# Heavy experts on quarters of TensorE's columns, in unsplit float32

## The chip, the cores and the metric

The kernel runs on one core of one Trainium2 chip. The metric is the device time of one execution in microseconds (us); lower is better. The core has TensorE (PE, matrix products), VectorE (DVE), ScalarE (ACT), GpSimd (POOL) and SyncE (SP, which here issues every DMA). TensorE writes to PSUM, which has eight banks of 128 rows by 512 float32.

## What is computed

Two layers of a transformer trunk over 256 latent and 256 context tokens of width 1024. The second layer ends in a mixture of eight experts, and the change lies there alone. In short:

```
logits = h @ router                       # h: 256 x 1024, eight logits a token
top_v, top_i = top_k(logits, 2)           # two experts a token
gates = softmax(top_v), put at top_i
for e in range(8):                        # w_gate, w_up: 1024 x 3584, w_down: 3584 x 1024
    out += gates[:, e:e+1] * ((silu(h @ w_gate[e]) * (h @ w_up[e])) @ w_down[e])
x = x + g2 * out;   return rms_norm(x, final_norm_g)
```

All arrays are float32. One expert's weights are 44 MB, all eight 352 MB; each is read once from HBM. With the inputs of `setup_inputs()` the reference routes 49, 84, 60, 51, 58, 61, 72 and 77 tokens to experts 0 to 7.

## The kernel before

The kernel first runs the mixer and the dense feed-forward part of layer 0, then the mixer of layer 1, then the expert stage (`moe`). The expert stage is the second half of the span.

**Places.** The eight experts are taken in eight places, `KIND = "LHLHHLHL"`. Place 0 is expert 0; the other experts are ranked by their number of tokens when the router's result is known, and ranks 1 to 4 go to the heavy places (H), the others to the light ones (L). A light place has 64 slots for tokens, a heavy one 128 (`CAP`). If an expert has more tokens than slots, `overflow` runs all experts a second time for the rest, in a branch at the end (`tc.If(n > 0)`, line 2390) that is otherwise jumped over by every engine. `slots` makes one-hot matrices of tokens against slots, and `gather` multiplies the tokens with them.

**Weights.** Loads are units of 1 MB, 42 for an expert, issued in order by SP, each into four slots of an arena of 104 slots (`SLOT`, `SLOTS`). The inner width of 3584 is cut into blocks of 1024, 1024, 1024 and 512 columns (`WIDE = (2, 2, 2, 1)`). For each block the gate and up products run over eight steps k of the contraction, the products are combined, transposed by TensorE (`flip`), and `down` multiplies them with rows of w_down into the banks `y`.

**Light places** multiply the float32 weights as they lie in the arena (`native`, `pairs`): the 64 slots are the stationary operand, the gate product goes to rows 0 to 63 of a bank, that is to the left half of the array's columns, and the up product to rows 64 to 127, the right half:

```
self.mm(p[0:64], xs[k], wg(kk, q), k == 0, k == KT - 1)
self.mm(p[64:128], xs[k], wu(kk, q), k == 0, k == KT - 1)
```

A float32 product shows in the trace as two MATMUL records.

**Heavy places** split every weight into a high and a low part in the short type float32r (`wunit`, `cut_next` on ScalarE, `cut_rest` on VectorE), likewise the tokens and the hidden block, and make three products of 128 columns each for one float32 product (`lin`: high by high, high by low, low by high). A split piece takes four more slots of the arena (up to `PIECES = 4` pieces at a time), and a load's slots come free when its split is done.

**Order.** The order on each engine is written by a planner (`drive`) that steps generators by prices of instructions (`mm`) and by the arena's free slots: `place_raw` admits a load while `held_raws * 4 + cut * 4 + live + 4 <= SLOTS - SPARE[self.ap]`, with `SPARE = (16, 26, 26)`. At run time the engines keep this order and wait for each other by semaphores; a load waits until the last reader of its slots is done.

**After an expert**, `slot_gates` puts the gates on the slots, `scaled` multiplies them onto `y` and splits the result, and `combine` spreads it back to the tokens with two products for each of four tiles.

Of the kernel before, what the change touches and what calls it, by code (L numbers as in the profile page):

```python
# [41 lines left out]
SLOT, SLOTS, FOURS, SPARE, ROOM = 512, 104, (5, 3), (16, 26, 26), 62  # L42
# [8 lines left out]
KIND, CAP = "LHLHHLHL", dict(H=128, L=64)  # L51
RANK = (0, 1, 5, 2, 3, 6, 4, 7)
WIDE = (2, 2, 2, 1)
# [81 lines left out]
class Arena:  # L135
# [18 lines left out]
    def take(self, n, dt=F32):  # L154
        i = len(self.uses)
        self.uses.append([n, self.count, self.count, dt == F32R])
        if self.rehearsal:
            s, self.top = self.top, self.top + n
            t = self.all[:, s * SLOT:(s + n) * SLOT].bitcast(dt)
        else:  # L160
            s, new = self.layout[i]
            four = s // 4
            if new:
                t = self.tiles[four] = self.pool.tile([128, 4 * SLOT], dt, name=f"four{four}", tag=f"four{four}")
                self.base[t.tensor.name] = four * 4, 4 * SLOT
            t = self.tiles[four][:, s % 4 * SLOT:(s % 4 + n) * SLOT]
        for k in range(n):
            self.at[s + k] = i
        return t


def lay_out(uses):
# [4 lines left out]
    for n, a, b, r in uses:  # L177
# [5 lines left out]
    for i in sorted(range(len(uses)), key=lambda i: (uses[i][1], -uses[i][0])):  # L183
        n, a, b, r = uses[i]
# [27 lines left out]
class Trunk:  # L212
# [37 lines left out]
    def act(self, dt=F32, name="a", n=1):  # L250
        self.live += n
        self.peak = max(self.peak, self.live)
        return self.arena.take(n, dt)
# [81 lines left out]
    def mm(self, out, lhsT, rhs, start=True, stop=True):  # L335
# [127 lines left out]
    def native(self, src, kts, cols):  # L463
# [3 lines left out]
        def w(k, q=0):  # L467
            c = k * cols + q * 512
            return u["raw"][:, c:c + 512]
# [56 lines left out]
    def load(self, u):  # L526
        u["raw"] = self.arena.take(4)
# [44 lines left out]
    def cut_next(self):  # L572
# [3 lines left out]
        p["h"], p["l"] = self.arena.take(2, F32R), self.arena.take(2, F32R)  # L576
# [238 lines left out]
    def mloads(self):  # L815
        while self.mfree and self.mnext < len(self.mseq):
            l, part, hf, k = self.mseq[self.mnext]
            t = self.arena.take(1)
# [996 lines left out]
    def moe_units(self):  # L1815
# [4 lines left out]
        def make(W, e, r, c, lie, ks):  # L1820
# [3 lines left out]
            w = self.native(src, kts, cols) if KIND[e] == "L" else self.wunit([src], kts, cols)  # L1824
# [3 lines left out]
        def gu(e, i):  # L1828
# [3 lines left out]
            two = [(w, g) for w in range(2) for g in range(0, KT, kts)]  # L1832
            if KIND[e] == "L":
                two.sort(key=lambda x: x[1])
            for w, g in two:
# [4 lines left out]
        def dn(e, i):  # L1840
            f0, n = sum(WIDE[:i]) * 512, WIDE[i] * 512
            us = [make(Dn, e, s(f0, f0 + n), s(0, D), "(p k) c -> p k c", s(g, g + 2)) for g in range(0, n // 128, 2)]
            return [(u, k) for u in us for k in range(2)]
# [141 lines left out]
    def slots(self, e, r=None, pe=None):  # L1985

        t = (self.OH if r is None else self.OHR)[e] = self.act(name="OH")
        io = self.io128
        if KIND[e] == "L":
            io = io[:, 0:64].unsqueeze(1).to_broadcast([128, 2, 64])  # L1990
        for tb in range(2):
            o = t[:, tb * 128:(tb + 1) * 128]
            if KIND[e] == "L":
                o = o.rearrange("p (a s) -> p a s", a=2)
            at = self.pe[:, tb, e:e + 1] if pe is None else pe[:, tb]
            if r is None:
                self.V.tensor_scalar(o, io, at, None, op0=OP.is_equal)
            else:
                self.V.tensor_scalar(o, io, at, r[:, tb:tb + 1], op0=OP.is_equal, op1=OP.mult)
# [8 lines left out]
    def gather(self, e, g, xe):  # L2008

        heavy = KIND[e] == "H"  # L2010
        n, ks = (128, range(g * 4, g * 4 + 4)) if heavy else (64, range(KT))
        p = self.ps("pxe")
        for i, k in enumerate(ks):
            for tb in range(2):
                self.mm(p[:, i * n:(i + 1) * n], self.xtok[tb][k // 4][:, (k % 4) * 128:(k % 4 + 1) * 128],
                        self.OHR[e][:, tb * 128:tb * 128 + n], tb == 0, tb == 1)
        last = not heavy or g == 1
        u = self.act(name="u")
        sl = [slice(i * n, (i + 1) * n) for i in range(len(ks))]
        col = [(self.modc[:, 1, 0, 3, k:k + 1], self.nA[:, 1, 1, 0, k:k + 1]) for k in ks]  # L2020
        v3 = lambda t: t.rearrange("p (k n) -> p k n", n=n)
        wide = lambda t: t.unsqueeze(2).to_broadcast([128, len(ks), n])
        hl = (self.act(F32R, "xeh"), self.act(F32R, "xel")) if heavy else None

        def scale():
            self.V.tensor_mul(v3(u), v3(p), wide(self.nA[:, 1, 1, 0, ks[0]:ks[0] + len(ks)]))
            self.V.tensor_add(v3(u), v3(u), wide(self.modc[:, 1, 0, 3, ks[0]:ks[0] + len(ks)]))
            if last:
                self.drop(1)

        def high():
            if e:
                self.S.copy(hl[0], u)
            else:
                for c, (sh, sc) in zip(sl, col):
                    self.S.activation(hl[0][:, c], p[:, c], AF.Identity, bias=sh, scale=sc)

        def low():
            self.V.tensor_sub(hl[1], u, hl[0].bitcast(F32))
            self.drop(1)  # L2040

        st = [(self.V, scale)]
        if heavy:
            st = (st + [(self.S, high)] if e else [(self.S, high)] + st) + [(self.V, low)]
        self.after(self.t + 196.0, *st, key=("xe", e, g), banks=1)
        xe += [(hl[0][:, c], hl[1][:, c]) if heavy else u[:, c] for c in sl]

    def slot_gates(self, e):

        p = self.ps("pgs")  # L2050
        for tb in range(2):
            self.mm(p[:, e:e + 1], self.OH[e][:, tb * 128:(tb + 1) * 128], self.gate[:, tb, e:e + 1], tb == 0, tb == 1)
        self.after(self.t + 196.0, (self.V, lambda: self.V.tensor_copy(self.gs[:, e:e + 1], p[:, e:e + 1])),
                   key=("gs", e), banks=1)

    def scaled(self, e, Y):

        g, ys = self.gs[:, e:e + 1], []
        if e == NE - 1:
            t = self.act(name="yg")  # L2060
            self.V.scalar_tensor_tensor(t, Y[0], g, self.g2l, op0=OP.mult, op1=OP.mult)
            return [(t,)] * 2

        def split(y, hh, hl):
            def free():
                self.V.scalar_tensor_tensor(hl, y, g, hh.bitcast(F32), op0=OP.mult, op1=OP.subtract)
                self.held -= 1
            return [(self.S, lambda: self.S.activation(hh, y, AF.Copy, scale=g)), (self.V, free)]

        for i, y in enumerate(Y):  # L2070
            hh, hl = self.act(F32R, "yh"), self.act(F32R, "yl")
            ys.append((hh, hl))
            self.after(self.t + 196.0, *split(y, hh, hl), key=("ys", e, i))
        return ys if len(ys) == 2 else ys * 2

    def combine(self, e, ys, hf, tb):

        p = self.ps("pcb")
        rows = slice(0, 128) if KIND[e] == "H" else slice(hf * 64, hf * 64 + 64)
        o = self.OHT[e][rows, tb * 128:(tb + 1) * 128]  # L2080
        if len(ys[hf]) == 1:
            self.mm(p, o.bitcast(F32), ys[hf][0][rows], True, True)
        else:
            self.mm(p, o, ys[hf][0][rows], True, False)
            self.mm(p, o, ys[hf][1][rows], False, True)
        if not e:
            self.tok[tb][hf] = self.act(name="tok")
        t = self.tok[tb][hf]
        if e == NE - 1:
            self.V.tensor_add(t, p, t)  # L2090
            return
        self.after(self.t + 196.0, (self.V, lambda: self.V.tensor_add(t, p, t)) if e else (self.S, lambda: self.S.copy(t, p)),
# [8 lines left out]
    def moe(self, J, R):  # L2101
# [14 lines left out]
        def to_oht(e):  # L2116
            p = self.ps("pot")
            for tb in range(2):
                c = slice(tb * 128, (tb + 1) * 128)
                self.tr(p[:, c], self.OH[e][:, c])  # L2120
            self.OHT[e] = self.act(F32R, "OHT")
            self.after(self.t + 196.0, (S, lambda: S.copy(self.OHT[e][:, 0:256], p[:, 0:256])), key=("oht", e), banks=1)
# [13 lines left out]
        wide = lambda name, j: [(name, j, q) for q in range(WIDE[J[j][1]])]  # L2136
        side = []
        self.gs = C.tile([128, 8], F32, name="gslot")
# [406 lines left out]
```

## Time and profile before

| | us |
|---|---|
| median of 3 runs | 1745.29 (1745.13 to 1747.17) |
| the profiled execution | 1749.87 |
| its span, first to last instruction | 1748.1 |
| TensorE busy | 1707.2 (98%) |
| VectorE busy | 1153.9 (66%) |
| ScalarE busy | 811.9 (46%) |

The profile's pages cut the span into 40 slices, so a slice is 43.7 us, and name a tile by the pool that it comes from: `four` is any piece of the arena, and `g`, `u`, `y`, `pht`, `pcb` are PSUM banks. Nearly every instruction has line 121, that of the recording helper, so groups are told apart by tile and shape. A shape 128*64 on TensorE is 128 rows by 64 columns of stationary operand. The expert stage's products run from 878 to 1734 us.

### The profile page before, as it was taken

To read this page: it belongs to the slowest core of one execution; us is meant where nothing else is said; L and a number is where in the kernel's file an instruction comes from. 1 tells how busy PE (TensorE), PEld (TensorE's weight loads), DVE (VectorE), ACT (ScalarE), POOL (GpSimd) and SP (SyncE) were. 2 spreads that over 40 slices of the span, in tenths; PEclk is the share of its full clock that TensorE was granted. 3 is DMA by queue.
4 is the path that set the end of the run, shared out by engine and by line. 5 is a ranking of instruction groups with operands and counts; after the bars stand their busy time and mean duration, and the time that the engine had idled before them with its cause. 6 is when DMAs were issued, how large, how long until landed. Compare 5 with 4: busy or idle time off the path is not lost. (4 is left out here: it accounts for less than half of the span.)

```text
span 1748.1 us, 22827 instructions
## 1 busy us (share of the span) xinstructions
PE 1707.2 (98%) x8291; PEld 1224.1 (70%) x8291; DVE 1153.9 (66%) x1928; ACT 811.9 (46%) x1388; POOL 1.1 (0%) x7
## 2 busy tenths in 40 slices
PE   8999998999999999999999999999999999999997
PEld 4876777788888888977834787446887864568632
DVE  6898988888874335588512796227999952489523
ACT  3467754433222223466402675126777741367412
POOL 0000000000000000000000000000000000000000
PEclk9899999999999998999989999999999999999999
DMA  9631244455883225116779999999999999999995
GB/s 306 209 120 53 79 139 139 146 172 179 290 289 97 83 76 173 63 59 217 265 291 410 375 374 369 414 407 413 409 366 349 390 356 413 409 411 409 392 411 232
DMA packets 191573, 469.97 MB, mean 269 GB/s; under 512 B 13632, under 2 KB 81756, under 8 KB 177116
## 3 DMA queue, kind: packets, MB, share of 16 engines
q1 hardware_dynamic: 191452, 468.42, 71.9%
q8 instruction: 67, 1.10, 0.3%
q14 instruction: 54, 0.44, 0.1%
HBM read 467.34 MB, written 1.05 MB: 268 GB/s over the span
## 5 line engine op out<-in xcount | busy, mean ns | idle before, releaser
L121 DVE TENSOR_TENSOR four<-four,four 128x1024 fp32r<-128x1024 f32 (+9 forms) x633 | 622.5, 1017 | 239.9 <-ACT four L121 199.0
L121 ACT CAST four<-four 128x1024 fp32r<-128x1024 f32 (+7 forms) x564 | 507.1, 934 | 432.3 <-PE pp L121 197.0
L121 PE MATMUL pp<-four,four 128*128 128x512 f32 (+1 forms) x2678 | 592.7, 381 | 4.4 <-ACT four L121 3.4
L121 PEld LDWEIGHTS pp<-four,four 128*128 128x128 f32 x2678 | 479.8, 191 | 100.5 <-ACT four L121 4.6
L121 PE MATMUL g<-four,four 128*64 128x512 f32 (+1 forms) x1532 | 370.0, 519 | 7.7 <-DVE four L121 6.4
L121 PEld LDWEIGHTS g<-four,four 128*64 128x64 f32 (+1 forms) x1532 | 176.5, 159 | 153.0 <-issue 112.5
L121 PE MATMUL y<-four,four 128*128 128x512 f32 (+1 forms) x1088 | 252.5, 474 | 0.7 <-DVE four L121 0.7
L121 PEld LDWEIGHTS y<-four,four 128*128 128x128 f32 (+1 forms) x1088 | 151.4, 167 | 90.6 <-issue 61.6
L121 PE MATMUL u<-four,four 128*128 128x512 f32 x630 | 151.6, 392 | 0.5 <-DVE four L121 0.5
L121 DVE SCALAR_TENSOR_TENSOR four<-four,sc,four 128x512 f32<-128x512 f32 x213 | 150.9, 747 | 0.9
L121 PEld LDWEIGHTS u<-four,four 128*128 128x128 f32 x630 | 117.5, 188 | 26.3 <-DVE four L121 2.2
L121 DVE TENSOR_TENSOR four<-four,g 64x512 f32<-64x512 f32 x28 | 19.2, 691 | 92.3 <-ACT four L121 92.3
L121 ACT ACTIVATE four<-g 64x512 f32<-64x512 f32 (+1 forms) x56 | 31.7, 592 | 103.8 <-PE g L121 103.6
L121 ACT ACTIVATE four<-psc,nm 128x512 f32<-128x512 f32 (+1 forms) x72 | 43.7, 614 | 20.5 <-DVE nm L121 15.2
L121 ACT COPY four<-pht 128x512 f32<-128x512 f32 (+1 forms) x16 | 8.5, 532 | 90.7 <-PE pht L121 90.7
L121 DVE TENSOR_REDUCE mx<-psc 128x1 f32<-128x512 f32 (+1 forms) x72 | 40.6, 597 | 5.4 <-PE psc L121 5.2
L121 ACT ACTIVATE four<-four 128x512 f32<-128x512 f32 x36 | 22.7, 630 | 45.2 <-DVE four L121 41.3
L121 DVE TENSOR_TENSOR four<-pcb,four 128x512 f32<-128x512 f32 x28 | 19.1, 690 | 36.5 <-PE pcb L121 36.5
L121 PE MATMUL psc<-four,four 128*128 128x512 f32 (+3 forms) x136 | 39.6, 422 | 1.2 <-ACT four L121 1.2
L121 PEld LDWEIGHTS pht<-idf,four 64*128 64x128 f32 (+1 forms) x224 | 28.6, 197 | 15.1 <-issue 10.8
L121 PE MATMUL po<-four,four 128*64 128x256 f32 x280 | 38.8, 392 | 0.2 <-ACT four L121 0.2
L121 DVE TENSOR_TENSOR four<-pht,four 128x512 fp32r<-128x512 f32 x28 | 18.2, 686 | 28.3 <-ACT four L121 27.9
(228 smaller groups left out, 1233.9 us busy)
## 6 DMA issues: line engine op xcount, KB each, us to landing
four<-in_moe_w_gate_dram SPq DMA_DIRECT2D x112, 1024.0 KB, 12.9
four<-in_moe_w_up_dram SPq DMA_DIRECT2D x112, 1024.0 KB, 13.8
four<-in_moe_w_down_dram SPq DMA_DIRECT2D x112, 1024.0 KB, 13.8
four<-in_w_mod_dram SPq DMA_DIRECT2D x192, 256.0 KB, 4.6
four<-in_ffn_w_down_dram SPq DMA_DIRECT2D x16, 704.0 KB, 4.8
four<-in_w_in_dram SPq DMA_DIRECT2D x10, 1024.0 KB, 6.3
four<-in_ffn_w_gate_dram SPq DMA_DIRECT2D x10, 1024.0 KB, 8.5
four<-in_ffn_w_up_dram SPq DMA_DIRECT2D x10, 1024.0 KB, 6.3
```

Of the source, the lines that this page charges most:

```text
L121: return None if arena.rehearsal else f(*args, **kw)
```

## The change

A heavy place gets 96 slots in place of 128, and its weights are no longer split: like a light place it multiplies the float32 weights from the arena. Its 96 slots are three groups of 32, each the stationary operand of one quarter of the array's columns; gate and up of two halves of a block make twelve products for one k, three rounds over the four quarters. The hidden block, `flip` and `down` follow the same layout, in light places too, where the two halves of a block are now stacked on 128 rows before the transposition. The gates are multiplied on the token side when `combine` adds to the tokens, so `slot_gates` goes; `scaled` only splits, stacked, and `combine` has one product a tile for a light place and two for a heavy one. w_down's rows are taken in halves of a block. `SPARE` becomes `(16, 16, 16)`. `overflow` gets two branches in place of one.

```diff
-KIND, CAP = "LHLHHLHL", dict(H=128, L=64)
+KIND, CAP = "LHLHHLHL", dict(H=96, L=64)
+LIE = dict(H=256, L=128)
-SLOT, SLOTS, FOURS, SPARE, ROOM = 512, 104, (5, 3), (16, 26, 26), 62
+SLOT, SLOTS, FOURS, SPARE, ROOM = 512, 104, (5, 3), (16, 16, 16), 62
...
             if lhsT.shape[-1] == 64:
                 c *= 0.56
+            elif lhsT.shape[-1] == 32 and n >= 256:
+                c *= 0.27
...
-            w = self.native(src, kts, cols) if KIND[e] == "L" else self.wunit([src], kts, cols)
+            w = self.native(src, kts, cols)
...
-            us = [make(Dn, e, s(f0, f0 + n), s(0, D), "(p k) c -> p k c", s(g, g + 2)) for g in range(0, n // 128, 2)]
-            return [(u, k) for u in us for k in range(2)]
+            us = [(make(Dn, e, s(f0 + q * n, f0 + q * n + n), s(0, D), "(p k) c -> p k c", s(g, g + 2)), q, g)
+                  for g in range(0, n // 128, 2) for q in range(2)]
+            return [(u, k, q, g + k) for u, q, g in us for k in range(2)]
...
-    def slot_gates(self, e):
...
+        def products(P, gate, up, xs, e, j):
+            n = WIDE[J[j][1]] * 256
             for k, ((wg, kk), (wu, _)) in enumerate(zip(gate, up)):
...
+                x, st, sp = xs[k], k == 0, k == KT - 1
+                step = 32 if KIND[e] == "H" else 64
+                for q in range(2):
+                    for r in range(0, 128, step):
+                        w = (wu, wg)[(r // 64 + q) % 2]
+                        self.mm(P[q][r:r + step, 0:n], x[:, r % 64:r % 64 + step], w(kk, q, n), st, sp)
+                if KIND[e] == "H":
+                    for r in range(4):
+                        self.mm(P[2][r * 32:r * 32 + 32, 0:n], x[:, 64:96], (wg, wu)[r // 2](kk, r % 2, n), st, sp)
...
+            step = 64 if light else 32
+            for f, (w, kk, q, k) in enumerate(R[j]["d"]):
...
+                for r in range(0, 128, step):
+                    c = k * 128 + q * 64 + r % 64
+                    self.mm(y[0][r:r + step], t[0][:, c:c + step], w(kk, r // 64), st, sp)
+                if not light and f % 2:
+                    for r in range(4):
+                        w2, k2, q2, f2 = R[j]["d"][f - 1 + r % 2]
+                        c = f2 * 64 + q2 * 32
+                        self.mm(y[1][r * 32:r * 32 + 32], t[1][:, c:c + 32], w2(k2, r // 2), i == 0 and f == 1, sp)
...
+        t, g = self.tok[tb][hf], self.gate[:, tb, e:e + 1]
+        add = lambda: self.V.scalar_tensor_tensor(t, p, g, t, op0=OP.mult, op1=OP.add)
...
-        with nullcontext() if n is None else tc.If(n > 0):
-            for e in range(NE):
+        for c in range(2):
+            with nullcontext() if n is None else tc.If(n > 128 * c):
+                for e in range(NE):
```

The first place of the order is TensorE at the start of the first heavy place (place 1). Before, with `four_7521` and `four_7567` the split tokens and the other numbers split weights:

```order
L121 MATMUL y<-four_7463,four_75 64x512 x4
L121 MATMUL g<-four_7358,four_7521 128x512 x2
L121 MATMUL g<-four_7517,four_7521 128x512 x2
L121 MATMUL g<-four_7358,four_7521 128x512 x2
L121 MATMUL pht<-idf,four_75 128x64 x4
L121 MATMUL g<-four_7546,four_7521 128x512 x6
L121 MATMUL g<-four_7550,four_7521 128x512 x6
```

The same place now, with `raw` a load's slots and `tok` the gathered tokens:

```order
L122 MATMUL y<-raw,xin 64x512 x16
L122 MATMUL g<-raw,tok 32x512 x24
L122 MATMUL pht<-idf,xin 128x128 x2
L122 MATMUL g<-raw,tok 32x512 x72
L122 MATMUL y<-raw,cols 64x512 x8
```

For each k and block of 1024, twelve split products on all 128 columns (six of gate here, six of up in a later pass) have become three rounds of four float32 products on 32 columns each, gate and up together, read straight from the loads.

The second place is SP, whose queue issues the loads, in the middle of the loads of the first heavy place. The names in brackets are the semaphores that a load waits for: DMAHW are earlier DMAs, PE_49, DVE_49 and Activation_49 the engines. Before:

```order
L121 DMA four_9057<-in_moe_w_down_dram 128x2048 [waits DMAHW2_49,DVE_49,PE_49]
L121 DMA four_9083<-in_moe_w_down_dram 128x2048 [waits DMAHW3_49,DVE_49]
L121 DMA four_9191<-in_moe_w_gate_dram 128x2x1024 [waits DMAHW6_49,DVE_49,Activation_49]
L121 DMA four_9200<-in_moe_w_gate_dram 128x2x1024 [waits DMAHW7_49,DVE_49]
L121 DMA four_9268<-in_moe_w_up_dram 128x2x1024 [waits DMAHW3_49,DVE_49]
```

The same loads now:

```order
L122 DMA raw<-in_moe_w_down_dram 128x2048 [waits DMAHW2_49,PE_49]
L122 DMA raw<-in_moe_w_down_dram 128x2048 [waits DMAHW3_49,PE_49]
L122 DMA raw<-in_moe_w_gate_dram 128x2x1024 [waits DMAHW6_49,PE_49]
L122 DMA raw<-in_moe_w_up_dram 128x2x1024 [waits DMAHW7_49,PE_49]
L122 DMA raw<-in_moe_w_gate_dram 128x2x1024 [waits DMAHW4_49,PE_49]
```

The loads waited for VectorE's split and now wait for TensorE's products, and gate and up loads alternate.

## Rows read from the trace of the kernel before

**Rows 1.** The page: the span, and its 40 slices of DMA share and rate.

```profile
span 1748.1 us, 22827 instructions
...
DMA  9631244455883225116779999999999999999995
GB/s 306 209 120 53 79 139 139 146 172 179 290 289 97 83 76 173 63 59 217 265 291 410 375 374 369 414 407 413 409 366 349 390 356 413 409 411 409 392 411 232
```

**Rows 2.** TensorE's timeline where a place starts: start us, us, engine, line, group, [idle].

```profile
878.43 8.28 PE L121 MATMUL g<-four,four 128*64 128x512 f32 x24 [1.51 <-DVE four L121]
...
960.72 1.45 PE L121 MATMUL g<-four,four 128*128 128x512 f32 x5
...
1085.18 2.37 PE L121 MATMUL g<-four,four 128*64 128x512 f32 x10
...
1172.90 1.65 PE L121 MATMUL g<-four,four 128*128 128x512 f32 x6
...
1426.98 2.37 PE L121 MATMUL g<-four,four 128*64 128x512 f32 x10
...
1515.34 1.65 PE L121 MATMUL g<-four,four 128*128 128x512 f32 x6
...
1643.84 2.37 PE L121 MATMUL g<-four,four 128*64 128x512 f32 x10
```

**Rows 3.** Stretches: us, busy (x) of PE, PEld, DVE, ACT, POOL, PEclk, DMA share, GB/s.

```profile
900.00:1725.00 825.00, 817.56 (x3802) 525.39 (x3800) 499.46 (x523) 408.76 (x470) 0.00 (x0) 1.00 1.00 394
1075.00:1275.00 200.00, 197.36 (x898) 119.92 (x897) 112.61 (x122) 90.20 (x104) 0.00 (x0) 1.00 1.02 410
1275.00:1425.00 150.00, 148.53 (x707) 124.38 (x707) 134.73 (x134) 108.81 (x119) 0.00 (x0) 1.00 0.93 358
1425.00:1625.00 200.00, 197.01 (x916) 120.07 (x915) 112.15 (x122) 89.85 (x105) 0.00 (x0) 1.00 1.03 411
1725.00:1730.00 5.00, 5.00 (x26) 1.79 (x27) 0.00 (x0) 1.66 (x2) 0.00 (x0) 1.00 0.29 120
```

**Rows 4.** Groups by shape, 878 to 1734 us: xcount | busy us, mean ns | idle before.

```profile
L121 DVE TENSOR_TENSOR four<-four,four 128x1024 fp32r<-128x1024 f32 x336 | 394.1, 1221 | 67.0 <-ACT four L121 62.2 <-DMA four<-in_moe_w_gate_dram 0.5 <-issue 0.4
L121 ACT CAST four<-four 128x1024 fp32r<-128x1024 f32 x336 | 339.7, 1052 | 133.0 <-PE g L121 59.0 <-PE y L121 35.5 <-PE u L121 25.5
L121 PE MATMUL g<-four,four 128*64 128x512 f32 x896 | 207.8, 605 | 1.5 <-DVE four L121 1.5
L121 PE MATMUL g<-four,four 128*128 128x512 f32 x636 | 162.2, 398 | 6.2 <-DVE four L121 4.9 <-ACT four L121 1.4
...
L121 DVE TENSOR_TENSOR four<-four,g 64x512 f32<-64x512 f32 x28 | 19.2, 691 | 92.3 <-ACT four L121 92.3
...
L121 ACT ACTIVATE four<-g 64x512 f32<-64x512 f32 x28 | 16.3, 588 | 101.5 <-PE g L121 101.5
```

**Rows 5.** What the queue of DMA issues (SPq) waited for longest, 878 to 1710 us: us, times, longest.

```profile
SPq L121 <- DVE four L121: 331.7, 135, 11.8
```

**Rows 6.** TensorE's timeline, dense runs: of halves (128*64), whole array, two columns.

```profile
1714.65 1.89 PE L121 MATMUL g<-four,four 128*64 128x512 f32 x8
...
1725.13 8.80 PE L121 MATMUL y<-four,four 128*64 128x512 f32 x40
...
1019.78 3.79 PE L121 MATMUL y<-four,four 128*128 128x512 f32 x16
...
14.43 4.45 PE L121 MATMUL pmod<-four,sc 128*2 128x512 f32 x10
...
256.12 2.81 PE L121 MATMUL po<-four,four 128*64 128x256 f32 x24
```

**Rows 7.** The tail: PE's instructions of line 2390, then the timeline.

```profile
L2390 PEldq COMPARE_BRANCH  x1: 3622/3622/3622, 1730.1 to 1730.1; - x1
L2390 PEldq EVENT_SEMAPHORE  x1: 51/51/51, 1734.0 to 1734.0; - x1
...
1734.08 0.75 DVE L121 SCALAR_TENSOR_TENSOR four<-y,gslot,four 128x512 f32<-128x512 f32 x1 [9.86 <-PEq L2390]
```

More of the change, by code (lines that the diff above doesn't have):

```diff
@@ L163, in take @@
             if new:
-                t = self.tiles[four] = self.pool.tile([128, 4 * SLOT], dt, name=f"four{four}", tag=f"four{four}")
+                t = self.tiles[four] = self.pool.tile([128, 4 * SLOT], dt, name=name, tag=f"four{four}")
                 self.base[t.tensor.name] = four * 4, 4 * SLOT
@@ L252, in act @@
         self.peak = max(self.peak, self.live)
-        return self.arena.take(n, dt)
+        return self.arena.take(n, dt, name)
     def nm(self, ap):
@@ L526, in load @@
     def load(self, u):
-        u["raw"] = self.arena.take(4)
+        u["raw"] = self.arena.take(4, F32, "raw")
         self.held_raws += 1
@@ L1831, in gu @@
             h = [[], []]
[L1832 to L1835, printed above, removed]
+            for w, g in [(w, g) for g in range(0, KT, kts) for w in range(2)]:
                 u = make((G, U)[w], e, s(0, D), s(f0, f0 + n), "(k p) c -> p k c", s(g, g + kts))
@@ L2027, in scale @@
             self.V.tensor_add(v3(u), v3(u), wide(self.modc[:, 1, 0, 3, ks[0]:ks[0] + len(ks)]))
-            if last:
+            if not heavy or g == 1:
                 self.drop(1)
[L2031 to L2046, printed above, removed]
-    def slot_gates(self, e):
[L2050 to L2054, printed above, removed]
+        self.after(self.t + 196.0, (self.V, scale), key=("xe", e, g), banks=1)
@@ L2056, in scaled @@
+        xe += [u[:, i * n:(i + 1) * n] for i in range(len(ks))]
     def scaled(self, e, Y):
-        g, ys = self.gs[:, e:e + 1], []
         if e == NE - 1:
             t = self.act(name="yg")
[L2061 to L2066, printed above, removed]
+            self.V.tensor_mul(t, Y[0], self.g2l)
+            return t
@@ L2067, in free, with stages, high, low @@
+        r, ys = (slice(0, 64), slice(64, 128)), []
+        def stages(y, hl):
+            def high():
+                for h in range(2):
+                    self.S.copy(hl[h][r[h]], y[r[h]])
+            def low():
+                for h in range(2):
+                    self.V.tensor_sub(hl[h][r[1 - h]], y[r[h]], hl[h][r[h]].bitcast(F32))
                 self.held -= 1
-            return [(self.S, lambda: self.S.activation(hh, y, AF.Copy, scale=g)), (self.V, free)]
+            return [(self.S, high), (self.V, low)]
@@ L2070, in scaled @@
         for i, y in enumerate(Y):
[L2071 to L2074, printed above, removed]
+            ys.append([self.act(F32R, "ys") for _ in range(2)])
+            self.after(self.t + 196.0, *stages(y, ys[i]), key=("ys", e, i))
+        return ys
     def combine(self, e, ys, hf, tb):
         p = self.ps("pcb")
-        rows = slice(0, 128) if KIND[e] == "H" else slice(hf * 64, hf * 64 + 64)
@@ L2134, in final_g @@
             fg.append(self.spread(self.cols[:, 38 + hf * 4:42 + hf * 4], "fg"))
[L2136 removed]
+        wide = lambda name, j: [(name, j, q) for q in range(3 if KIND[J[j][0]] == "H" else 2)]
         side = []
[L2138 removed]
         Y, hids, hT = {}, {}, {}
```

320 lines of the change are left out of this document (128 added, 192 removed).

## The prediction

> **What bounds the kernel now.** The page's slices come first: in the second half of the span the DMA share is 9 tenths at 349 to 414 GB/s [rows 1], so the expert stage runs near the loads' limit, and only there does the change act; in the built program TensorE's instructions are in the same order up to the first transposition of place 0. Then the starts of the places on TensorE [rows 2]. Their differences are the places' lengths: L 82.3, H 124.5, L 87.7, H+H 254.1, L 88.4, H 128.5, and the last L 90.2 up to 1734.0, the end of its products [rows 7]. The light places sum to 348.6 us, the heavy ones to 507.0, all to 855.6. Against this stand 42 loads of 1.049 MB, 44.0 MB a place, which at the 410.5 GB/s of the two stretches of 200 us [rows 3] take 107.3 us. So a heavy place (126.8 on average) is slower than its loads and a light one (87.1) faster. What a light place gains it can use only as far as loads run ahead of it, and in the two heavy places in a row the rate falls to 358 [rows 3]: the arena is full there and loads wait, above all for VectorE [rows 5], whose second halves of the splits free their slots (336 at 1.2 us [rows 4]). From 900 to 1725 the rate is 394 on average; TensorE waits little (6.2 us before heavy g, 1.5 before light g [rows 4]). So TensorE's work bounds the stage, and the loads stand 4% behind it.
>
> **TensorE, heavy places.** Removed: for each k and block of 512 columns six split products, with down 504 in a place, at 0.227 us (16 in 3.79 us: (3.79 - 0.39)/15, with 0.39 for the last alone [rows 4, 6]) = 114.3 us; the other 12.5 us of a place are transpositions, gathers, combinations and waits. Added: 552 float32 products of one quarter, 96 of them of width 256, in time as much as 504 of width 512; two records each (light g has 448 products and 896 records [rows 4]), so 1008 records of full width. What four records on four quarters take together no row shows. The bounds: a record on two columns with nothing beside it takes 0.429 us ((4.45 - 0.59)/9, with 0.59 for the last alone), as long as a pair on the two halves: 40 records in 8.80 us are 19 steps of 0.429 and the last pair's 0.6 [rows 6]. So a second tile costs no step, and at width 256 neither (24 in 2.81: 11 steps of 0.22 [rows 6]). The upper bound is 0.215 a record, a quarter no better than a half; the lower 0.107, four in one step. I take 0.107, by the nearest row: from one tile to two the step stayed the same. 1008 x 0.10725 = 108.1 us. The other 12.5 us I leave: waits for splits go, changes of tiling around each transposition come. A heavy place: 120.6, the four 24.6 us less than now.
>
> **TensorE, light places.** Halves are stacked, so the transpositions are half as many, the gates' products go, and combination halves: some 2.5 us a place, 10 in all, of 87.1. The last block works at width 256, which the row of width 256 shows to be as dense. Sum: 348.6 - 10 + 4 x 120.6 = 821 us, from 878.4 to **1699.4**.
>
> **Loads.** The same 336 units in packets of the same size. What moves is when they may start. Following, in the built programs, each load's waits back to the load whose reader they name, the distance is 10 to 12 loads in heavy places before and 18 to 20 everywhere now: no split pieces, and smaller `SPARE`. Twenty loads are 51 us at 2.55 us each, more than the two heavy places in a row fall behind, 2 x (120.6 - 107.3) = 27 us; place 1 falls 13 behind and place 2 makes it good. So the loads should not stop. The bytes after 900 us: 825 x 394 + 5 x 120 = 325.7 MB [rows 3], at 410.5 GB/s 793.4 us, to 1693.4; two steps of down behind the last load, some 3.5 us, end at **1697**. TensorE's 1699 and the loads' 1697 are so near that I take the later. VectorE and ScalarE lose 394 and 340 us of split work [rows 4] and bound nothing. An eviction is 0.59 us on ScalarE and 0.69 on VectorE [rows 4]; three of them, pipelined, some 2.7 us, lie beside eight steps of 1.3 us of down. If that cover were gone, they would show in 16 heavy blocks: 43 us.
>
> **The tail.** Before, TensorE's branch takes 3.6 us from 1730.1 and lies beside the last products; its semaphore instruction at 1734.0 lets VectorE go at 1734.08 [rows 7]. The second branch is queued behind that instruction, which waits for the last product, and VectorE's next step waits for the second one's: nothing covers it. Between 0.05 (the semaphore's own row) and 3.6 us; I take 3.6, the row of the same instruction on the same engine. It is not entered: the heavy places get 84, 77, 72 and 61 tokens, the light ones at most 60. The rest of the tail, 1748.1 - 1734.0 = 14.1, stays.
>
> **Sum.** 1699.4 + 3.6 + 14.1 = 1717.1 us of span, 31.0 less. Around the span lie 1.8 us, and the profiled execution's 1749.87 is 4.6 above the median of the runs; 1717.1 + 1.8 - 4.6 = **1714**.
>
> **Rival 1, slower: fewer than four quarters at once.** Place: the 4032 quarter records of the four heavy places. Each ns above 107.25 costs 4.0 us, so at 115 the gain of 31 is gone: the point from which it decides. If a quarter's second record holds up the next quarter's first, two run at once, at 0.215: 4032 x 0.107 = 432 us more, 2146. For it: in the program the two records of a product follow each other on one tile. Against it: in that order 8 records on halves would take four steps and the last record, 2.3 us; they take 1.89 [rows 6], three steps and the last pair. There the second tile passes the first one's waiting record.
> The Trainium skill ("TensorE: Matmul & The Clock Gate", Part 3: Packing small matmuls) says that products start and end strictly in program order, which here would mean the 2146; the row of 1.89 us disagrees with it for two tiles. The same part measured three column tiles at 2.38 times one tile. At that 0.79 of full packing a heavy place's products would take 136.8 us in place of 108.1, and the end, an estimate, would be 1714 + 115 = 1829; no row here shows three or four tiles.
> Two at once gets 0.06. Any other packing under 93% of full, which also ends slower, gets 0.11: TensorE would have to start a weight load or a product every 54 ns, where halves ask for one every 107 (two records, four instructions, in 0.429), and four streams of float32 would be read at once.
>
> **Rival 2, dearer quarters.** 109 to 114 ns: each load of weights or change of tiling adds a little. At 111, 4 x 4.03 = 15 us: 1729. For it: heavy g is not free of waits now (6.2 us [rows 4]). Its range is 1725 to 1741; 0.14.
>
> **Rival 3, no change: the loads do not speed up.** If 394 GB/s is what the memory gives while TensorE streams four quarters, 325.7 MB end at 1726.7, and with 3.5 + 3.6 + 14.1 the span is 1747.9. Against it: 410 and 411 over 200 us with TensorE as busy [rows 3]. 0.05.
>
> **How the numbers follow.** The forecast has 0.64: its own range 1702 to 1724, from loads at 413 GB/s and no cost of the branch to 109 ns a record. The range 1702 to 1741 adds rival 2 and holds some 0.78. Faster by over 0.2% (3.5 us, about what a measurement of this kernel tells from no change): 0.64 + 0.14 = 0.78; within: 0.05; slower: 0.17.
>
> **What would show it.** Right: 1104 quarter records a heavy place (192 of them of half width), in steps of 0.43 us for four; heavy places of 115 to 122 us; 405 to 413 GB/s in every slice from 900 us on; no 128x1024 splits; the last products near 1699; a second branch of some 3.6 us before VectorE's last scaling. Wrong: steps over 0.46 us for four (rivals 1, 2), or slices under 400 GB/s while loads wait for TensorE. The forecast fails first on the packing, which rests on pairs alone.

## The result, and the profile after

The changed kernel takes 1719.49 us (median of 4 runs, 1717.4 to 1721.12) where the kernel before takes 1745.21 (4 runs, 1744.37 to 1747.17): a ratio of 0.985, with a 95% interval of 0.9833 to 0.9867. It is 1.5% faster. Its profiled execution took 1717.4 us, 1715.6 of them in the span. The forecast was 1714, its range 1702 to 1741.

The page of the changed kernel, its span, the busy time of three engines and the slices of 42.9 us, answers to [rows 1]:

```profile
span 1715.6 us, 26672 instructions
...
PE 1672.5 (97%) x10727; PEld 983.4 (57%) x10727; DVE 763.2 (44%) x1599; ACT 489.8 (29%) x1083; POOL 1.1 (0%) x7
...
DMA  8731244366893226125679999999999999999994
GB/s 300 233 114 54 81 141 142 112 194 186 268 309 109 85 75 195 36 88 181 240 276 408 413 408 411 413 408 413 407 412 412 407 413 401 412 412 404 413 406 172
```

The loads run at 401 to 413 GB/s in every slice from the 22nd to the last but one; before they fell to 349 and 356. VectorE and ScalarE lost 391 and 322 us of work, about the splits of [rows 4]. Where the places start on TensorE (start us, us, then the group; 128*32 is a quarter of the array's columns) answers to [rows 2]:

```profile
874.14 7.74 PE L122 MATMUL g<-raw,tok 128*64 128x512 f32 x24 [1.51 <-DVE tok L122]
...
953.70 5.36 PE L122 MATMUL g<-raw,tok 128*32 128x512 f32 x48
...
1072.15 3.65 PE L122 MATMUL g<-raw,cols 128*64 128x512 f32 x16
...
1158.11 5.36 PE L122 MATMUL g<-raw,xin 128*32 128x512 f32 x48
...
1398.17 3.65 PE L122 MATMUL g<-raw,xin 128*64 128x512 f32 x16
...
1484.14 5.36 PE L122 MATMUL g<-raw,xin 128*32 128x512 f32 x48
...
1602.60 3.65 PE L122 MATMUL g<-raw,tok 128*64 128x512 f32 x16
...
1692.09 1.94 PE L122 MATMUL y<-raw,tok 128*64 128x512 f32 x8 [0.42 <-SPq L2335]
...
1701.93 3.48 PE L122 MATMUL pcb<-xin,OHT 64*128 64x512 f32 x8 [7.90 <-DVE xin L122]
```

The places now take L 79.6, H 118.4, L 86.0, HH 240.1, L 86.0, H 118.5 and L 91.4 us, 819.9 in all up to the end of the last product at 1694.0: the heavy ones 477.0 (119.2 each; 507.0 before), the light ones 342.9 (348.6 before). 48 quarter records take 5.36 us, twelve steps of 0.429 and the last four's tail. Then, from 1694.0 to 1701.9, TensorE does nothing. The stretches (us, busy of PE, PEld, DVE, ACT, POOL, granted clock, DMA share, GB/s) answer to [rows 3]; the last two lie in the tail:

```profile
900.00:1690.00 790.00, 788.08 (x6244) 291.06 (x6242) 108.26 (x190) 86.54 (x165) 0.00 (x0) 1.00 1.02 408
1275.00:1425.00 150.00, 150.00 (x1344) 53.12 (x1332) 21.53 (x40) 17.29 (x34) 0.00 (x0) 1.00 1.02 411
1696.00:1700.00 4.00, 0.00 (x0) 0.00 (x0) 0.00 (x0) 0.00 (x0) 0.00 (x0) 0.77 0.05 8
1700.00:1704.00 4.00, 2.07 (x6) 1.05 (x8) 0.69 (x1) 0.00 (x0) 0.00 (x0) 0.50 0.02 4
```

In the stretch of the two heavy places in a row where the loads had 358 GB/s they now keep 411 (its last 27 us lie in a light place; the two heavy places alone, from 1158 to 1398, have 410). And TensorE's sequencer at the line of the branches (ns as least/median/most, then first and last start) answers to [rows 7]; the row under it is VectorE's first step of the tail:

```profile
L2335 PEldq COMPARE_BRANCH  x2: 3379/4063/4747, 1692.7 to 1696.3; - x2
L2335 PEldq EVENT_SEMAPHORE  x2: 51/51/51, 1696.1 to 1701.1; - x2
...
1701.18 0.69 DVE L122 TENSOR_TENSOR xin<-y,tok 128x512 f32<-128x512 f32 x1 [19.54 <-PEq L2335]
```

Two branches in a row, 3.4 and 4.7 us, and VectorE starts 0.03 us behind the second one's semaphore. Before, one branch of 3.6 us lay beside the last products. So the expert stage gave what was forecast, and the tail took some of it.

One thing has to be known for the rest: the part of the program ahead of the expert stage, the same in all these kernels, ends in one execution earlier than in another. In the profiles of the changed kernel and the eleven below, the first place starts between 873.7 and 879.2 us. Medians of a few runs therefore carry some 2 us either way, and effects of a few us are read from the first place's start to the end of the span: 869.7 us before (1748.1 - 878.4), 841.5 in the changed kernel (1715.6 - 874.1). The run with another `SPARE` below, in which nothing of the stage changed, gives 841.9.

### The profile page after: what moved, and what is told of

It reads as the page before. It is cut to its first block, busy times and chain, and to the rows that moved or that the text cites. A ratio compares the mean times of both kernels' runs of the same rounds, so it can differ in the third digit from the quotient of the medians.

```text
span 1715.6 us, 26672 instructions
## 1 busy us (share of the span) xinstructions
PE 1672.5 (97%) x10727; PEld 983.4 (57%) x10727; DVE 763.2 (44%) x1599; ACT 489.8 (29%) x1083; POOL 1.1 (0%) x7
## 5 line engine op out<-in xcount | busy, mean ns | idle before, releaser
L122 PE MATMUL pp<-hh,wl 128*128 128x512 f32 (+2 forms) x1386 | 321.8, 387 | 1.8 <-ACT hh L122 1.5
L122 PEld LDWEIGHTS pp<-hh,wl 128*128 128x128 f32 (+1 forms) x1386 | 255.7, 189 | 55.0 <-ACT hh L122 1.9
L122 PE MATMUL g<-raw,tok 128*32 128x512 f32 (+3 forms) x2048 | 254.7, 544 | 2.3 <-DVE tok L122 1.5
L122 PEld LDWEIGHTS g<-raw,tok 128*32 128x32 f32 (+1 forms) x2048 | 82.9, 117 | 148.1 <-issue 129.5
L122 DVE TENSOR_TENSOR wl<-raw,wl 128x1024 fp32r<-128x1024 f32 (+5 forms) x116 | 116.5, 1018 | 99.0 <-ACT wl L122 65.6
L122 ACT CAST wl<-raw 128x1024 fp32r<-128x1024 f32 (+5 forms) x122 | 105.2, 885 | 189.3 <-PE pp L122 178.4
L122 PE MATMUL g<-raw,xin 128*32 128x512 f32 (+3 forms) x1024 | 127.3, 542 | 0.0
L122 PE MATMUL g<-raw,cols 128*32 128x512 f32 (+3 forms) x1024 | 125.6, 541 | 0.0
L122 PE MATMUL pp<-wl 128*128 128x512 f32 (+2 forms) x545 | 122.7, 362 | 2.2 <-ACT wl L122 1.5
L122 PEld LDWEIGHTS pp<-wl 128*128 128x128 f32 (+1 forms) x545 | 93.6, 192 | 18.2 <-ACT wl L122 1.9
```

Of the source, the lines that this page charges most:

```text
L122: return None if arena.rehearsal else f(*args, **kw)
```

## The experiments

### What the packing rests on

The twelve products for one k go round the four quarters. Two runs keep the products and change their order: by quarter (g = 32), or in pairs of quarters (g = 64).

```diff
-                for q in range(2):
-                    for r in range(0, 128, step):
...
+                for r0 in range(0, 128, g if KIND[e] == "H" else 128):
+                    rs = range(r0, r0 + g if KIND[e] == "H" else 128, step)
+                    for q in range(2):
+                        for r in rs:
+                            w = (wu, wg)[(r // 64 + q) % 2]
+                            self.mm(P[q][r:r + step, 0:n], x[:, r % 64:r % 64 + step], w(kk, q, n), st, sp)
+                    if KIND[e] == "H":
+                        for r in rs:
+                            self.mm(P[2][r:r + 32, 0:n], x[:, 64:96], (wg, wu)[r // 64](kk, r // 32 % 2, n), st, sp)
```

By quarter:

> The same twelve products for each k, ordered by quarter in the heavy places: three in a row on the first quarter, then three on the second, and so on (the changed kernel goes round the four quarters). It tells what the four in one step of 0.429 us rest on. Theory (each quarter holds its own waiting records, but the products come in program order and few can wait): the three products of a quarter, six records, take 6 x 0.43 = 2.6 us with only the ends of neighbours together, so 24 records take 9 us in place of 2.57 and the four heavy places some 700 us more: 2300 to 2450 us. Rival 1, the quarters run freely, in any order: 1719. Rival 2, a few products look ahead: in between, 1900 to 2200.

In pairs:

> The same twelve products in pairs of quarters: six that alternate between the first two quarters, then six that alternate between the last two. Theory (who is together is set by the neighbours in program order): two at once, 0.215 us a record in gate and up, so 24 records take 5.1 us in place of 2.57, which over 28 steps of 512 columns' worth in each of four places is 288 us more: 1980 to 2030 us, with down's products still four at once. Rival, the quarters run freely: 1719.

Measured, one run each: 1892.6 us by quarter, 1749.5 in pairs. Runs of 24, 48 and 144 records of the same place on TensorE, in the changed kernel, by quarter and in pairs:

```profile
959.42 15.66 PE L122 MATMUL g<-raw,tok 128*32 128x512 f32 x144
978.59 5.36 PE L122 MATMUL g<-raw,tok 128*32 128x512 f32 x48
985.18 2.78 PE L122 MATMUL g<-raw,tok 128*32 128x512 f32 x24
```

```profile
963.00 23.19 PE L122 MATMUL g<-raw,tok 128*32 128x512 f32 x144
989.71 8.98 PE L122 MATMUL g<-raw,tok 128*32 128x512 f32 x48
999.93 5.43 PE L122 MATMUL g<-raw,tok 128*32 128x512 f32 x24
```

```profile
960.17 16.54 PE L122 MATMUL g<-raw,tok 128*32 128x512 f32 x144
980.22 6.24 PE L122 MATMUL g<-raw,tok 128*32 128x512 f32 x48
987.70 3.66 PE L122 MATMUL g<-raw,tok 128*32 128x512 f32 x24
```

Both came out between the two ends, so the theory fell (it wanted 9 and 5.1 us for 24 records) and so did a wholly free order; by quarter the second rival holds in kind, 7 us below its range. What 24 more records cost is read from a long run less a short one: (15.66 - 5.36)/4 = 2.575 us round the quarters, (23.19 - 8.98)/4 = 3.55 by quarter, (16.54 - 6.24)/4 = 2.575 in pairs. One rule fits all three: products leave in program order, one product can wait at each quarter while another runs there, and a product that finds the place taken holds up all behind it. By quarter, the third of a quarter's three products leaves when the second starts, 0.86 us in, and only then the next quarter's first; so three quarters run side by side, three products end every 0.86 us, and twelve take 3.43. In pairs the second pair starts 0.86 us behind the first, then all four run; only the start and the end of a run lose 0.88 us (3.66 against 2.78). Round the quarters nothing is lost. The starts of the single records in the traces follow the rule: of the 24 at 999.93 us by quarter, 1, 1, 2, 2, 3, 3, 3, 3, 2, 2, 1 and 1 start in twelve steps of 0.43 us, and of the 24 at 987.70 in pairs, 2, 2, 4, 4, 4, 4, 2 and 2 in eight. By quarter each next quarter's first record starts 0.889 us behind the last one's and not 0.858, which makes the 3.55. The records don't name their quarter, so which of them belongs to which is argued, and whether the waiting place holds one product or that many records these runs don't tell.

### What sets the pace of the stage

Two runs take work away from one side only. The first leaves out the loads of w_up:

```diff
-                u = make((G, U)[w], e, s(0, D), s(f0, f0 + n), "(k p) c -> p k c", s(g, g + kts))
+                u = u if w else make(G, e, s(0, D), s(f0, f0 + n), "(k p) c -> p k c", s(g, g + kts))
...
-                    wu.done()
```

> The loads of w_up are left out: the up products read the gate's weights, so the expert stage does the same products with 28 loads a place in place of 42. What is left is TensorE's own pace. Theory (TensorE and the loads are near balance, the loads end last): of the stage's 819.9 us only the waits before products of halves, some 7 us by the steps that are longer than 0.43, go; TensorE runs ahead of its last products again, so that the first branch is hidden: 1708 to 1712 us, heavy places still of 118 to 120 us. Rival 1, the loads set the pace throughout and TensorE's steps hide it: under 1700. Rival 2, TensorE alone sets it: 1717 to 1720.

Measured 1714.4 us (1713.0 to 1717.5). The places sum to 816.5 us (875.9 to 1692.35), heavy ones again 118.5 to 120.0. The stretch of the stage, with the loads at 264 GB/s:

```profile
900.00:1690.00 790.00, 790.00 (x6256) 292.29 (x6254) 108.20 (x190) 85.87 (x164) 0.00 (x0) 1.00 0.72 264
```

So TensorE alone needs 816.5 us and waits for loads cost the changed kernel 3.4, not the 7 that I had read from long steps; the time lies above the forecast by that and a branch of 4.5 us that stayed in the open.

The second run leaves most of the third round out of TensorE's work, and leaves the loads as they are:

```diff
-                if KIND[e] == "H":
+                if KIND[e] == "H" and k == 0:
                     for r in range(4):
-                        self.mm(P[2][r * 32:r * 32 + 32, 0:n], x[:, 64:96], (wg, wu)[r // 2](kk, r % 2, n), st, sp)
+                        self.mm(P[2][r * 32:r * 32 + 32, 0:n], x[:, 64:96], (wg, wu)[r // 2](kk, r % 2, n), True, True)
...
-                if not light and f % 2:
+                if not light and i == 0 and f == 1:
                     for r in range(4):
...
-                        self.mm(y[1][r * 32:r * 32 + 32], t[1][:, c:c + 32], w2(k2, r // 2), i == 0 and f == 1, sp)
+                        self.mm(y[1][r * 32:r * 32 + 32], t[1][:, c:c + 32], w2(k2, r // 2), True, True)
```

> Of the third round of quarters (slots 64 to 95) the heavy places keep only the first step of each block, so experts with more than 64 tokens lose part of their contribution; loads as in the changed kernel. TensorE has some 34 us less in each of four places, 135 in all. Theory (loads end last in the changed kernel): weights keep coming at 408 to 412 GB/s, the last load's packet lands at 1689 to 1694 as in the changed kernel (1691.6), and the time is 1716 to 1721. Rival: TensorE set the pace and the loads followed it; then the time falls by 30 us and more, down to 1585.

Measured 1716.9 us (1715.3 to 1719.1), as the theory has it. The stretch and what TensorE waited for (us, times, longest) show the other side at its limit:

```profile
900.00:1690.00 790.00, 691.19 (x4942) 253.54 (x4940) 107.51 (x190) 84.50 (x164) 0.00 (x0) 0.97 1.02 409
```

```profile
PE g L122 <- DMA raw<-in_moe_w_up_dram: 90.3, 49, 4.5
PE y L122 <- DMA raw<-in_moe_w_down_dram: 7.8, 15, 1.2
```

Once the first buffered units are used up, light and heavy places alike take 107 to 108.6 us, 42 loads at 409 GB/s, and the stage 818.5 us (875.6 to 1694.15). TensorE alone 816.5, the loads alone 818.5, both together 819.9: a gain on one side would meet the other within 4 us.

A third run was to start the loads later, by the bound on the planner's loads:

```diff
-SLOT, SLOTS, FOURS, SPARE, ROOM = 512, 104, (5, 3), (16, 16, 16), 62
+SLOT, SLOTS, FOURS, SPARE, ROOM = 512, 104, (5, 3), (32, 32, 32), 62
```

> SPARE is (32, 32, 32) in place of (16, 16, 16): 16 slots, that is four loads, fewer may be on their way or waiting, before the expert stage begins too. In the changed kernel the loads stand still from 870 to 882 us, with the arena full, until the first products free slots. Theory (the loads end last, by a hair): four loads at 2.55 us have to come after 882 instead of before 870, so the last packet lands some 10 us later and the time is 1726 to 1731, with no slice under 400 GB/s after it. Rival: TensorE sets the pace and catches the loads up: 1718 to 1721. Rival 2, fewer loads on their way also slow the rate (slices under 400 GB/s): over 1735.

Measured 1718.6 us (1717.4 to 1722.2), no change. But the dose did not reach: summed over the packets of the trace, 329.3 MB of the weights were still to come when the first place started, in this run and in the changed kernel alike. So it says nothing on what a later or earlier start of the loads would do; that stays open, with the part of `SPARE` in the change.

### What the branches cost

One branch for both rounds of the overflow, behind the last product:

```diff
-        for c in range(2):
-            with nullcontext() if n is None else tc.If(n > 128 * c):
+        with nullcontext() if n is None else tc.If(n > 0):
+            for c in range(2):
                 for e in range(NE):
```

> The changed kernel with both rounds of the overflow inside one branch, taken or jumped over once. In the profile of the changed kernel TensorE's two branch instructions take 3.4 us (from 1692.7) and 4.7 us (from 1696.3), its last product ends at 1694.0, and VectorE's next step starts at 1701.2. Theory: from 1694.0 on TensorE's branches are all that the tail waits for, so one branch less ends 4.9 us earlier (4.75 and 0.15 between them): 1714.6 us against 1719.5, with VectorE's first scaling some 2 us behind the last product. Rival: something else holds the tail (a bank, a semaphore of another engine) and the branches lie beside it: 1719.5, and the gap stays at 7.

Measured 1719.9 us (1716.4 to 1721.5): nothing won. From the first place to the end it takes 840.2 us against 841.5. The branch and TensorE's next rows:

```profile
L2334 PEldq COMPARE_BRANCH  x1: 3839/3839/3839, 1697.0 to 1697.0; - x1
...
1696.41 1.94 PE L122 MATMUL y<-raw,tok 128*64 128x512 f32 x8 [0.43 <-SPq L2334]
...
1704.33 3.79 PE L122 MATMUL pcb<-xin,OHT 64*128 64x512 f32 x8 [5.98 <-issue]
```

VectorE did start early, 1701.0, 2.65 us behind the last product. But TensorE, whose operand was ready at 1701.7, started at 1704.33 with no wait that the profile shows ("issue"). In the trace's DMA records two packets of 16 KB on a queue of instructions fall here, at 1698.1 and at 1701.5. That fits a TensorE that is without instructions; the records don't say whose packets they are. So the branch was not the whole cost, and I had priced the wrong thing.

The same branch ahead of the last down products:

```diff
+        self.overflow()
         yield from down(len(J) - 1)
-        self.overflow()
```

> One branch, and it stands before the down products of the last block of the last place in place of behind them. There TensorE waits for the last loads in any case (records in groups of eight with 0.4 to 0.6 us between them, from 1684 to 1692). Theory: the branch lies beside the wait for the loads and the tail starts right behind the last product: 7.1 us less than the changed kernel, 1712.4 us. Rival: TensorE's halt of 3.4 us goes straight to the end, since the loads were not what it waited for: 1715 to 1718.

Measured 1717.6 us (1712.2 to 1720.2), first place to end 839.3. The theory (1712.4) fell. The last load's packet landed at 1693.6, so most of the branch did lie beside the loads; what it left behind did not. TensorE's timeline behind it, and the stretch 1696 to 1700 us:

```profile
1694.74 6.55 PE L122 MATMUL y<-raw,tok 128*64 128x512 f32 x16 [3.70 <-PEq L2334]
```

```profile
1696.00:1700.00 4.00, 4.00 (x12) 1.16 (x10) 0.00 (x0) 0.00 (x0) 0.00 (x0) 0.50 0.00 0
```

The branch took 4.6 us, from 1689.7. Behind it 16 records, which take some 3.6 us at full clock, take 6.55: TensorE had stood idle for 3.70 us, and the clock granted it from 1696 to 1700 is 0.50, the level of 1.2 GHz in place of 2.4. Waits of 0.4 to 0.6 us just ahead left it at 1.00.

The branch still earlier, ahead of the last 20 down products:

> One branch, and it stands inside the down products of the last place, ahead of its last 20 products (40 records, 8.6 us), where TensorE has records queued. One branch behind the last product and one ahead of the last eight gave 1719.9 and 1717.6 us: in both TensorE stood idle for 3.7 us and more, went on at half its pace (0.85 us for a pair of records on halves in place of 0.43), and fetched instructions before its first step. Theory: as in the kernel before (branch from 1730.1, products until 1734.0), some 3.9 us of queued records cover the branch, so TensorE halts for about 1 us, keeps its clock, and the tail starts right behind the last product: 1712 to 1715 us. Rival: the halt is longer than the cover and the slow clock eats what is won: 1716 to 1719.

```diff
                     flip(j + 1)
+                    yield self.when(("hT", j + 1, 0), *[("res", hf, tb) for tb, hf in both])
+                    self.overflow()
```

Measured 1718.8 us (1716.1 to 1719.7), first place to end 838.4; the rival, 1716 to 1719, holds. TensorE's branch, and its timeline behind it:

```profile
L2335 PEldq COMPARE_BRANCH  x1: 6027/6027/6027, 1684.4 to 1684.4; - x1
...
1690.62 6.70 PE L122 MATMUL y<-raw,tok 128*64 128x512 f32 x24 [5.58 <-PEq L2335]
```

Beside loads at 304 GB/s (from 1684.4 to 1690.4) the branch took 6.0 us; nothing was queued ahead of it, since TensorE had just waited for a transposition's input. So this run doesn't test the cover that its theory wanted.

The price of all of it, the overflow left out (its call removed):

> The overflow and its branches are left out altogether (no expert here has more tokens than slots, so it is never entered). It prices all that the branches cost the changed kernel: the wait from the last product to VectorE's scaling (7.1 us in its profile), and the slow clock of the first products behind the wait. Theory: nothing else lies between, so the scaling starts within 0.1 us of the last product, TensorE keeps its full clock, and the execution ends 7 to 8 us earlier: 1711 to 1713 us. Rival: the tail's chain of VectorE and ScalarE has slack of its own that eats part of it: 1714 to 1717.

Measured 1709.8 us (1708.9 to 1711.0; ratio to the kernel before 0.979, 0.9773 to 0.9806), first place to end 833.4: 8.1 us less than the changed kernel (9.7 by the medians; the theory had 7 to 8). TensorE's last products and the first of the tail:

```profile
1693.76 1.94 PE L122 MATMUL y<-raw,xin 128*64 128x512 f32 x8 [0.43 <-DMA raw<-in_moe_w_down_dram]
1696.49 1.99 PE L122 MATMUL pcb<-cols,OHT 64*128 64x512 f32 x8 [0.79 <-DVE cols L122]
```

The same eight records of `pcb` take 1.99 us here and 3.48 in the changed kernel, at half the clock.

Why is a branch so dear on TensorE, and 0.05 to 0.07 us on the others, as on VectorE in the changed kernel?

```profile
L2335 DVEq COMPARE_BRANCH  x2: 56/64/72, 1681.8 to 1686.5; - x2
```

One branch over a short body:

```diff
-                for e in range(NE):
+                for e in range(1):
...
-                    for i in range(7):
+                    for i in range(1):
```

> One branch, and behind it a body of 56 instructions of TensorE in place of 3635 (one expert and one block of the overflow are left in; the rest of it, which these inputs never enter, is left out). It tells whether the branch is dear by itself or by the distance that it jumps. In the profiles so far a packet of 16 KB of instructions is read while TensorE's branch lasts, and another one a few us later. Theory (the distance: the target has to be fetched): the branch takes under 0.3 us, as on the other engines (0.05 to 0.07), and the time is 1712 to 1714. Rival (a branch drains the engine's queue, whatever its distance): 3.4 us and more, and 1718 to 1720 as with one branch and the long body.

And one branch over the long body, with a hint on TensorE:

```diff
+                    if not self.arena.rehearsal:
+                        self.tc.mark_branch_hint_location("over", "LikelyTaken", [mybir.EngineType.PE])
...
-            with nullcontext() if n is None else tc.If(n > 128 * c):
+        with nullcontext() if n is None else tc.If(n > 0, label="over"):
```

> One branch behind the last product, with the long body, and a hint to TensorE's instruction prefetch that this branch is likely to be taken; in the built program the hint stands at the start of TensorE's instructions. Theory (the fetch of the target is what the branch takes): if the hint is kept until then, the branch takes under 0.5 us and the time is 1712 to 1715. Rival: a hint so far ahead is lost: as with one branch, 1718 to 1721.

Measured: 1712.1 us (1708.5 to 1714.9) over the short body, 1712.5 (1710.1 to 1716.3) with the hint; first place to end 833.9 and 834.1. TensorE's branch over the short body; then, with the hint, the hint itself, the branch and the tail:

```profile
L2334 PEldq COMPARE_BRANCH  x1: 375/375/375, 1698.2 to 1698.2; - x1
```

```profile
L2481 PEldq BRANCH_PREFETCH_HINT  x1: 50/50/50, 0.8 to 0.8; - x1
...
L2336 PEldq COMPARE_BRANCH  x1: 410/410/410, 1698.0 to 1698.0; - x1
...
1697.41 1.94 PE L122 MATMUL y<-raw,tok 128*64 128x512 f32 x8 [0.43 <-SPq L2336]
...
1699.49 0.69 DVE L122 TENSOR_TENSOR xin<-y,tok 128x512 f32<-128x512 f32 x1 [12.33 <-PEq L2336]
...
1700.23 1.99 PE L122 MATMUL pcb<-xin,OHT 64*128 64x512 f32 x8 [0.88 <-DVE xin L122]
```

The 3.84 us of one branch become 0.38 when the jump is short (a little over the 0.3 of the theory), and 0.41 when the far target was announced 1.7 ms ahead: the branch waits for the instructions at its target. A drain of the queue, the rival, would have taken as long over the short body. The 2.6 us of "issue" are gone too: TensorE starts 0.05 us behind its operand. The Trainium skill ("Runtime: NRT & Kernel Launch", Instruction fetch mechanics) says that a taken branch whose target is not among the pages already read halts until it has been fetched. These two runs agree. The run with the hint computes all that the changed kernel does, in 1712.5 us, a ratio to the kernel before of 0.9805 (0.978 to 0.9829), and is the fastest complete version here.

## Why the prediction held, and where it was off

**The bound.** Read as TensorE first, the loads 4% behind it; in the changed kernel the two were to end within 2 us of each other (1699 and 1697). They do, in the other order: TensorE alone takes 816.5 us, the loads alone 818.5, so the loads end last. The balance was right, and it is why the gain stops where it stops. That the stage's sum came within 1.1 us (819.9 for 821.0) is in part luck: the heavy places took 5.4 us less than forecast and the light ones 4.3 more.

**Heavy places.** The one number that no row showed, four records to a step, was taken by the nearest row as 0.107 us a record; measured are 2.575/24 = 0.1073. The products of a heavy place come to some 110 us by their steps (108.1 forecast), the rest to some 9 (12.5), a place to 119.2 (120.6). Before, TensorE was busy for all but 7.4 of 825 us [rows 3], so most of the 35.7 us that the stage lost is work of TensorE and not waits. Rival 1 had 17%; its first form rested on the order of a product's two records. The row of 1.89 us in [rows 6], which spoke against it, told the truth: a second tile's record does pass a first one's that waits. The Trainium skill ("TensorE: Matmul & The Clock Gate", Part 3: Packing small matmuls) states strict program order for starts and ends, and 2.38 for three column tiles. The traces agree with neither: round the quarters the first records of four products start within 0.02 us, 0.43 us ahead of any second one, and four quarters did four times the work of one. Taken for whole products and not for records, the strict order would fit the changed kernel, but not the run by quarter: there only the ends of neighbours could overlap, some 6.9 us for twelve products (an estimate, four times two products of 0.86), where 3.55 are measured. That run also shows how near the danger was: the same products written quarter by quarter cost 173 us.

**Light places.** Forecast 338.6 us; 339.5 without the w_up loads (79.6, 86.0, 86.0, 88.0), so 9.1 of the 10 us for stacking came. With all loads 342.9: 3.4 us of waits, in the last place.

**Loads.** Forecast at 410.5 GB/s, the last step's products to end at 1697. After 900 us came some 322 MB at 408 GB/s (325.7 forecast), the last packet at 1691.6 and the last products at 1694.0, 2.4 us behind it (3.5 forecast).

**The tail: the step that failed.** It counted 3.6 us for the second branch and nothing for the first, which "lies beside the last products". That cover came from products queued at TensorE, and they were there because TensorE was late. In the changed kernel TensorE waits for the last loads, nothing is queued, and the first branch stands in the open too: 2.1 us of it, then 5.0 for the second (4.7 of its own), and then half the clock for the first products of the tail, 0.9 us (from VectorE's first step to the end 14.4, with the hint 13.5). That is 8.0 us, the 21.6 from the last product to the end against 13.6 without the overflow; the forecast had 3.6 + 14.1 = 17.7. Where TensorE did run ahead, without the w_up loads, the first branch (3.5 us from 1688.5) lay beside products again, which ended at 1692.35. The sum said "If that cover were gone" of the evictions, and did not ask it here.

**The offset.** I took 4.6 us off, since the profiled execution of before lay that much above its median. The start of the first place goes with the clock granted to TensorE ahead of the stage. One stretch there, before and in the changed kernel:

```profile
680.00:720.00 40.00, 40.00 (x187) 36.37 (x187) 24.53 (x68) 16.32 (x34) 0.00 (x0) 0.79 0.25 78
```

```profile
680.00:720.00 40.00, 40.00 (x197) 36.77 (x198) 26.94 (x70) 15.78 (x32) 0.00 (x0) 0.86 0.18 60
```

The four profiles with a start at 877.8 to 879.2 us (before, one branch, short body, hint) have 0.79 or 0.80 there, the nine with one at 873.7 to 876.0 have 0.83 to 0.87. So the excess of before lay ahead of the expert stage, most of it at least, and is a matter of the single execution; the changed kernel's profile lies 2.1 us below its median, with a first place at 874.1. With these, 876.2 (874.1 + 2.1) + 819.9 + 7.15 + 14.4 + 1.8 = 1719.5, against 873.8 + 821.0 + 3.6 + 14.1 + 1.8 = 1714: the start 2.4 us, the tail 3.9, the stage -1.1.

Rival 2 (109 to 114 ns) did not come: the steps are at the prediction's lower bound. (At 4.0 us a ns its range starts at 1721; the prediction has 1725.) Rival 3, no faster loads, fell with 401 to 413 GB/s in every full slice.

## What to carry to other kernels

Small products on separate column tiles of TensorE (here float32, four tiles of 32 columns) run side by side without loss if neighbours in program order go round the tiles; grouped by tile they lose. A cost that is hidden beside queued work has to be priced again when the change makes its engine wait: the queue that hid it was a sign that the engine was late. A jump over a long body on TensorE costs several us, and then a slow clock, where no queued products lie beside it; give it a hint, or keep the body short.

## What was not expected of the hardware

TensorE's branch takes 3.4 to 6.0 us over a body of thousands of its instructions and 0.38 over one of 56; a hint that runs at 0.8 us, ahead of all of TensorE's products and some 1.7 ms ahead of its branch, still brings the 3.84 down to 0.41. After an idle time of 3.7 us TensorE's granted clock is 0.50 for the next several us (16 records in 6.55 us where some 3.6 are usual), while waits of 0.4 to 0.6 us leave it at 1.00. And a product whose quarter is taken holds up the products of other quarters behind it only when another one already waits there; that is the rule that the three orders fit.
